# Retention gates: which are projected by four-by-seven blocks, where the retained output is scaled, and how PSUM is divided in the retention stage

## The chip, the core and the metric

The kernel runs on one core of one Trainium2 chip. The metric is device time in microseconds; lower is better. The engines that matter are TensorE (PE in the profile, with its weight loads as PEld), VectorE (DVE), ScalarE (ACT), GpSimd (POOL) and SyncE (SP, which here only issues DMAs). Each works through its own instructions in program order and waits on the others by semaphores.

## The reference

The block is a decoder layer for 1024 tokens of width 1024, in float32. What matters here is the retention branch of its token mixer (4 heads, query and key width 256, value width 512, chunks of 128 tokens):

```python
s = jnp.einsum('bhid,bhjd->bhij', qi, ki) * inner_decay[None]
o = (jnp.einsum('bhij,bhje->bhie', s, vi)
     + jnp.einsum('bhid,bhde->bhie', qi, state) * q_decay[None, :, :, None])
state = (state * chunk_decay[None, :, None, None]
         + jnp.einsum('bhjd,bhje->bhde', ki * k_decay[None, :, :, None], vi))
...
mu = jnp.mean(ro, axis=-1, keepdims=True)
var = jnp.mean(jnp.square(ro - mu), axis=-1, keepdims=True)
ro = (ro - mu) * lax.rsqrt(var + GN_EPS)
ro = ro * gn_g + gn_b
ret_out = (jax.nn.silu(rg) * ro) @ w_ret_out
```

`rg` is a projection of the normed input by 2048 columns: 512 for each head, that is four blocks of 128 channels by 1024 tokens for each head, sixteen in all. Around it stand a dilated attention branch with its own projections, two sigmoid gates, an output projection and a squared-ReLU MLP.

## The kernel before

**Products.** Every float32 product is made of three passes of TensorE over halves of higher and lower precision (`mm3`, L203: low weight times high data, high times low, high times high). Nearly every matmul is 128 by 128 weights against 512 columns.

**Two ways to project.** A block of 128 channels can be projected directly: eight steps over the input width, each of three passes over two halves of the tokens, so 48 matmuls (`proj_mm`, L472). Or two such blocks are done together as a two-by-two block product with seven products instead of eight (class `Blocks`, L226). Each of the seven products has four steps of three passes, so a pair takes 84 matmuls where the direct way takes 96. Those pairs run in the stage `queries_keys` (L1259), one after the other in the order of the string at L1159: `r` retention queries and keys, `a` attention queries, `g` gates, `k` keys, `s` retention gates. For each product `prep` sums weight blocks on DVE and splits them on ACT and DVE, and `post` combines PSUM banks on ACT and DVE. A finished pair goes to DRAM. From `MOD0` on, `mod_turn` (L1243) also loads one modulation column block at a time and reduces it on DVE.

**The retention stage.** `chunk` (L715) runs 32 times, g = 0 to 31, four heads h of eight chunks c. In the order written out by hand, a chunk does on PE: the two `kv` products of the state (six matmuls); some steps of a direct gate projection (`rg_mm`, L695; the table `RG` gives how many steps each chunk takes, and one step is six matmuls); the scores of the next chunk and its transposed keys (`s_kt`, L630); the output `o` (three or nine matmuls); the four transposes of the chunk before (`on_T`, L670); and one last gate step. Around these:

- `kv` is added to the state on DVE (L745), copied to its high half on ACT (L749) and its low half on DVE (L750).
- the scores go through ACT and DVE (L652 to L668), the keys through ACT (L663) and DVE (L666).
- `o` goes through mean and variance on DVE (L772, L773), a scale and shift on DVE (L774), a power on POOL (L775), another product on DVE (L776), and DVE then writes the scaled output `on` (L778).
- `on_T` transposes `on` on PE and four ACT copies (L679) put it in tiles of 128 channels by 1024 tokens.
- `u_final` (L681) runs in the first four chunks of the next head: for each of four channel blocks two ACT instructions with scale and bias (L688), one DVE product with the gate (L690), one DMA (L691). For the last head it runs inside the first attention step (`att_step`, L1831), with its DMAs on POOL's queue.
- `ahead` prepares the next chunk's gate weights, if it has any: an ACT cast (L197) and a DVE subtraction (L198), and the load of a later weight block.

Twelve of the sixteen gate blocks are projected here, three for each head; the other four are two `s` pairs, and `rg_out` (L705) loads one of them for each head.

**PSUM.** There are eight banks of 512 float32 columns. In the retention stage two slots `mm` of two banks hold gate projections, and four slots `s` of one bank take in turn the scores, the transposed keys, the two `kv`, `o` and the transposes.

Of the kernel before, what the change touches and what calls it, by code (L numbers as in the profile page):

```python
# [17 lines left out]
P = 128  # L18
# [21 lines left out]
CS_KDEC = 128  # L40
CS_QD = 132
CS_QD2 = 136
CS_ONE = 140
# [97 lines left out]
def block_kernel(ctx, tc, io, stop=None, dbg=None):  # L141
# [11 lines left out]

    def banks(single):

        if PS:
            PS["ctx"].close()
        PS["i"] = PS.get("i", 0) + 1
        PS["ctx"] = ExitStack()
        PS["p"] = PS["ctx"].enter_context(tc.tile_pool(name=f"psum{PS['i']}", bufs=2, space=bass.MemoryType.PSUM,  # L160
                                                       reuse_waits="tile"))
        PS["n"] = 8 if single else 4

    banks(True)

    def ps_mm(name):
        return PS["p"].tile([P, 2, 512], F32, tag="mm", bufs=2, name=name)

    def ps_s(name, shape=(P, 512)):
# [342 lines left out]
    def etile(name, dt=F32):  # L512
        return R["p"].tile([P, 1024], dt, tag="E", bufs=12, name=name)

# [114 lines left out]

    def s_kt(i):  # L630

# [5 lines left out]
        for i in range(2):  # L637
# [27 lines left out]
        if pk is not None:  # L665
            nc.vector.scalar_tensor_tensor(flat(kl), flat(pk), kd, fv(flat(kh)), op0=ALU.mult, op1=ALU.subtract)  # L666
            hd["k", g] = (kh, kl)
        nc.vector.tensor_sub(sml, sm, fv(smh))  # L668

    def on_T(h, c):  # L670

        po = ps_s(f"oT{h}{c}", (P, 4, P))
        on = hd["o", h, c]
        if c == 0:
            hd["on", h] = [etile(f"on{h}{e}") for e in range(4)]
        for e in range(4):
            nc.tensor.transpose(po[:, e, :], on[:, e * P:(e + 1) * P], ident)
        for e in range(4):
            nc.scalar.copy(hd["on", h][e][:, c * C:(c + 1) * C], po[:, e, :])  # L679

    def u_final(h, es=range(4), queue=nc.sync):  # L681
        for e in es:
            i = h * 4 + e
            t = hd["on", h][e]
            for hf in range(2):
                neg = 16 if hf == i % 2 else 0
                b = t[:, 512 * hf:512 * hf + 512]
                nc.scalar.activation(b, b, AF.Identity, scale=gnv[0][:, neg + i:neg + i + 1],  # L688
                                     bias=gnv[1][:, neg + i:neg + i + 1])
            nc.vector.tensor_mul(t, t, hd["srg", h, e])  # L690
            queue.dma_start(y_d[h][:, 2 * (i % 2):2 * (i % 2) + 2, e // 2], t.rearrange("p (t x) -> p t x", t=2))  # L691

    RG = ((6, 2, 2, 3, 3, 3, 3, 2),) + ((3,) * NC,) * (H - 1)

    def rg_mm(n):  # L695

        for _ in range(n):
            if hd.get("rgk", NK) == NK:
                hd["rgk"], hd["rgw"], hd["rgp"] = 0, hd["rgws"].pop(0), ps_mm("rg")
            proj_mm(hd["rgp"], hd["rgw"], [hd["rgk"]])  # L700
            hd["rgk"] += 1
            if hd["rgk"] == NK:
                hd["rgs"] = hd["rgp"]

    def rg_out(h, c):  # L705

        if "rgs" in hd:
            e = {1: 0, 2: 0, 4: 1, 5: 1, 7: 2}[c]
            hd["srg", h, e] = etile(f"srg{h}{e}")
            nc.scalar.activation(hd["srg", h, e], flat(hd.pop("rgs")), AF.Silu)  # L710
        if c == 6:
            hd["srg", h, 3] = etile(f"srg{h}3")
            nc.sync.dma_start(hd["srg", h, 3], srg_d[h])

    def chunk(h, c, ahead, w=None):  # L715
# [19 lines left out]
        if g == 0:  # L735
            s_kt(1)
        rg_mm(1 if g == 0 else RG[h][c] - 1)
        for i, kv in enumerate(kvs):
# [5 lines left out]
            else:  # L744
                nc.vector.scalar_tensor_tensor(st[:, i, :], st[:, i, :], float(GAMMA[h] ** C), kv,  # L745
                                               op0=ALU.mult, op1=ALU.add)
        if g > 0:
            for i in range(len(kvs)):
                nc.scalar.copy(sh1[:, i, :], st[:, i, :])  # L749
                nc.vector.tensor_sub(sl1[:, i, :], st[:, i, :], fv(sh1[:, i, :]))  # L750
# [15 lines left out]
        if g > 0:  # L766
            on_T(*divmod(g - 1, NC))
        rg_mm(0 if g == 0 else 1)
        bn = p.tile([P, 6], F32, tag="bn", bufs=2, name=f"bn{h}{c}")
        ba = p.tile([P, 2], F32, tag="ba", bufs=2, name=f"ba{h}{c}")  # L770
        gr = p.tile([P, 1], F32, tag="gr", bufs=2, name=f"gr{h}{c}")
        nc.vector.bn_stats(bn, po)  # L772
        nc.vector.bn_aggr(ba, bn)  # L773
        nc.vector.tensor_scalar(gr, ba[:, 1:2], ct[:, CS_QD2 + h:CS_QD2 + h + 1], GN_EPS, op0=ALU.mult, op1=ALU.add)  # L774
        nc.gpsimd.tensor_tensor(gr, gr, mhalf[:, 0:1], op=ALU.pow)  # L775
        nc.vector.tensor_mul(gr, gr, ct[:, CS_QD + h:CS_QD + h + 1])  # L776
        on = p.tile([P, DV], F32, tag="on", bufs=1, name=f"onm{h}{c}")
        nc.vector.tensor_scalar(on, po, ba[:, 0:1], gr, op0=ALU.subtract, op1=ALU.mult)  # L778
        hd["o", h, c] = on
        rg_out(h, c)  # L780
        if h > 0 and c < 4:
            u_final(h - 1, (c,))

# [6 lines left out]
    ak_d = {(p, a): dram.tile([P, S], F32, name=f"akd{p}{a}") for p in range(2) for a in range(2)}  # L790
    srg_d = [dram.tile([P, S], F32, name=f"srgd{h}") for h in range(H)]
    h12_d = [dram.tile([P, 2, 512], F32, name=f"h12d{m}") for m in range(4)]
# [332 lines left out]
    def sums_of_h(name, ms=range(4)):  # L1125

        for m in ms:
# [18 lines left out]
            if name != "t4":  # L1146
# [42 lines left out]
    def a_out(q, n, x, y=None):  # L1189
# [19 lines left out]
        if n in ("12", "21"):  # L1209
            if pair[0] == "g":  # L1210
                dst = gate_d[GATES[2 * pair[1] + i]]
            elif pair[0] == "a":
                dst = aq_d[pair[2], pair[1], i]
            elif pair[0] == "k":
                dst = ak_d[pair[2], i]
            elif pair[0] == "s":
                dst = srg_d[2 * pair[1] + i]
            else:
                return
            nc.sync.dma_start(dst, OA[q][i])  # L1220
# [163 lines left out]
    def values(ahead):  # L1384
# [47 lines left out]
    steps.add(queries_keys, manual=True)  # L1432

    for h in range(H):
        for c in range(NC):
            steps.add((lambda h, c: lambda ahead, *w: chunk(h, c, ahead, *w))(h, c),
                      ([wsplit(io["w_rg"][3 * h + (0, 2, 5).index(c)])] if c in (0, 2, 5) else []),
                      manual=True)
# [392 lines left out]
    def att_step(pair, a):  # L1831

        def body(*args):
            ps = ps_mm(f"ak{pair}1{a}")
            gen = with_sums(proj_gen(ps, args[-1]))
            if a == 1:
                weave(gen, NK, scores_gen(pair, 1, 0), len(SB[1]), lag=2)
            elif pair == 0:
# [4 lines left out]
                drain(gen)  # L1843
                u_final(H - 1, queue=nc.gpsimd)
                for h in range(H):
# [982 lines left out]
def _constants():  # L2828
# [9 lines left out]
    for h in range(H):  # L2838
        lg = math.log(GAMMA[h])
        decay[:, h * C:(h + 1) * C] = \  # L2840
            np.where(i[None, :] >= i[:, None], np.exp(-lg * (i[:, None] + 1)), 0.0) / 16.0
        cst[:, CS_KDEC + h] = np.exp(lg * (C - 1 - i)) / 16.0
        cst[:, CS_QD + h] = np.exp(lg * (i + 1))
        cst[:, CS_QD2 + h] = np.exp(2 * lg * (i + 1))
    cst[:, CS_ONE] = 1.0
# [18 lines left out]
def pack(x, c, w_ada, b_ada, norm1_g, w_in, rel_bias, ret_gn_g, ret_gn_b,  # L2864
# [16 lines left out]
        "w_rv": _vblocks(w[:, 2048:4096]),  # L2881
        "w_rg": _cols(w[:, 4096:6144].reshape(1024, 4, 4, P)[:, :, :3].reshape(1024, 1536)),
        "w_rg2": _pairs(w[:, 4096:6144].reshape(1024, 4, 4, P)[:, :, 3].reshape(1024, 512)),
        "w_aq": _pairs(att[:, :, 0].reshape(1024, 1536)),
# [32 lines left out]
```

## Time and profile before

| what | us |
|---|---|
| time, median of the runs | 2175.16 |
| lowest | 2175.04 |
| the profiled execution's own time | 2173.28 |
| its span, first to last instruction | 2171.3 |
| PE busy | 2144.7 |
| DVE busy | 1520.4 |
| ACT busy | 959.3 |
| POOL busy | 165.7 |

The profile has one row for each instruction with its start and its duration. A row of PE is longer than the time until the next matmul may start, because matmuls are pipelined: how fast PE goes is read from the distance between starts. A group row adds up all instructions of one line, operands and shape: busy microseconds, mean nanoseconds of one, and the idle time of the engine just ahead of them with what ended it.

### The profile page before, as it was taken

How to read it: one execution, taken by the hardware profiler on the slowest of the kernel's cores; microseconds unless marked ns; L12 is line 12 of the kernel's file. 1: busy time of each engine (PE TensorE's matmuls, PEld its weight loads, DVE VectorE, ACT ScalarE, POOL GpSimd, SP SyncE). 2: the span in 40 equal slices, each digit the busy share in tenths (PEclk: the TensorE clock that was granted, in tenths of full speed). 3: DMA queues.
4: the chain of work that ended last, by engine and by line, in shares of the span. 5: the costliest groups of instructions: out<-in, count | busy, mean ns of one | idle time of the engine just before them, and what ended most of it. 6: DMA issues, size and time to landing. Idle time of an engine off the chain costs nothing. (4 is left out here: it accounts for less than half of the span.)

```text
span 2171.3 us, 27289 instructions
## 1 busy us (share of the span) xinstructions
PE 2144.7 (99%) x10036; PEld 1782.4 (82%) x10036; DVE 1520.4 (70%) x2358; ACT 959.3 (44%) x1757; POOL 165.7 (8%) x199
## 2 busy tenths in 40 slices
PE   8999999999999999999999999999999999999998
PEld 6888888888887788888888888888778888888887
DVE  6886777777656677776667644677876665877855
ACT  5543322323334455556656625434454455533413
POOL 0001111100001112211110000001000000000003
PEclk9999999999999999999999999999999999999999
DMA  9859998835588744436877366653144435645322
GB/s 383 282 208 309 285 306 265 243 117 194 186 301 303 234 148 151 160 127 197 218 194 196 115 245 211 217 191 132 64 175 160 150 136 193 253 135 173 109 88 78
DMA packets 162674, 425.18 MB, mean 196 GB/s; under 512 B 28005, under 2 KB 55916, under 8 KB 159468
## 3 DMA queue, kind: packets, MB, share of 16 engines
q1 hardware_dynamic: 150264, 374.90, 48.3%
q0 software_dynamic: 9584, 48.24, 9.9%
q8 instruction: 79, 1.29, 0.2%
q10 hardware_dynamic: 2692, 0.30, 0.1%
q14 instruction: 55, 0.45, 0.1%
HBM read 324.13 MB, written 160.32 MB: 223 GB/s over the span
## 5 line engine op out<-in xcount | busy, mean ns | idle before, releaser
L207 PE MATMUL qap<-hh,qaw 128*128 128x512 f32 x264 | 102.7, 389 | 0.0
L209 PE MATMUL qap<-hl,qaw 128*128 128x512 f32 x264 | 102.7, 389 | 0.0
L211 PE MATMUL qap<-hh,qaw 128*128 128x512 f32 x264 | 102.7, 389 | 0.0
L617 POOL TENSOR_TENSOR j<-qk,j 128x512 fp32r<-128x512 f32 x32 | 42.8, 1338 | 454.8 <-ACT j L616 454.8
L2235 POOL TENSOR_TENSOR accnf<-accnf,sqnf 128x256 f32<-128x256 f32 (+1 forms) x18 | 16.6, 922 | 609.6 <-ACT sqnf L2231 609.6
L2339 ACT ACTIVATE a<-a 128x512 f32<-128x512 f32 x48 | 30.3, 631 | 72.8 <-DVE a L2338 71.3
L749 ACT CAST stateh<-state 128x512 fp32r<-128x512 f32 x54 | 32.9, 622 | 57.8 <-DVE state L745 55.7
L209 PEld LDWEIGHTS qap<-hl,qaw 128*128 128x128 f32 x264 | 49.5, 188 | 10.4
L211 PEld LDWEIGHTS qap<-hh,qaw 128*128 128x128 f32 x264 | 49.6, 188 | 10.3
L207 PEld LDWEIGHTS qap<-hh,qaw 128*128 128x128 f32 x264 | 49.5, 188 | 10.2
L2547 ACT CAST w2h<-w2s 128x512 fp32r<-128x512 f32 x36 | 22.4, 621 | 80.3 <-DVE w2s L2585 80.3
L264 DVE TENSOR_TENSOR fw<-w1r,fw 128x512 fp32r<-128x512 f32 x48 | 32.9, 688 | 33.6 <-ACT fw L254 33.6
L264 DVE TENSOR_TENSOR qaw<-wa,qaw 128x512 fp32r<-128x512 f32 x66 | 44.0, 687 | 9.4 <-ACT qaw L254 9.4
L2070 DVE TENSOR_TENSOR rwl<-rwl,rwh 128x1024 fp32r<-128x1024 f32 x25 | 30.2, 1221 | 29.0 <-ACT rwh L2100 29.0
L207 PE MATMUL fp<-h2h,fw 128*128 128x512 f32 x128 | 50.0, 390 | 0.0
L209 PE MATMUL fp<-h2l,fw 128*128 128x512 f32 x128 | 49.8, 389 | 0.0
L211 PE MATMUL fp<-h2h,fw 128*128 128x512 f32 x128 | 49.8, 389 | 0.0
L207 PE MATMUL roa<-rh,rwl 128*128 128x512 f32 x128 | 49.8, 389 | 0.0
L209 PE MATMUL roa<-rl,rwh 128*128 128x512 f32 x128 | 49.8, 389 | 0.0
L211 PE MATMUL roa<-rh,rwh 128*128 128x512 f32 x128 | 49.8, 389 | 0.0
L1603 ACT ACTIVATE P<-P,ng 128x128 f32<-128x128 f32 (+1 forms) x96 | 41.9, 438 | 17.6 <-DVE ng L1595 17.5
L292 DVE TENSOR_TENSOR qat<-qat,qap 128x512 f32<-128x512 f32 x22 | 15.1, 688 | 42.8 <-PE qap L211 35.8
(3089 smaller groups left out, 7187.8 us busy)
## 6 DMA issues: line engine op xcount, KB each, us to landing
cossin<-in_w_ada_dram SPq DMA_DIRECT2D x32, 512.0 KB, 3.5
v<-vd SPq DMA_DIRECT2D x32, 512.0 KB, 4.3
w1r<-in_w_ff_dram SPq DMA_DIRECT2D x32, 512.0 KB, 4.6
yt<-y POOLq DMA_DIRECT2D x24, 512.0 KB, 7.5
xsd<-as SPq DMA_DIRECT2D x24, 512.0 KB, 3.1
w2r<-in_w_ff2s_dram SPq DMA_DIRECT2D x24, 512.0 KB, 6.4
em<-in_w_ada_dram SPq DMA_DIRECT2D x16, 512.0 KB, 10.2
wrvs<-in_w_rv_dram POOLq DMA_DIRECT2D x16, 512.0 KB, 9.8
```

Of the source, the lines that this page charges most:

```text
L207: nc.tensor.matmul(o, wl, xh, start=first, stop=False, skip_group_check=skip)
L209: nc.tensor.matmul(o, wh, xl, start=False, stop=False, skip_group_check=skip)
L211: nc.tensor.matmul(o, wh, xh, start=False, stop=last, skip_group_check=skip)
L264: nc.vector.tensor_sub(t[:, 512:], src, fv(t[:, :512]))
L292: nc.vector.tensor_sub(u, u, b)
L617: nc.gpsimd.tensor_sub(t[:, 1], src, fv(t[:, 0]))
L749: nc.scalar.copy(sh1[:, i, :], st[:, i, :])
L1603: nc.scalar.activation(v, v, AF.Exp, bias=ng[:, blk:blk + 1], accum_out=st[:, g, blk, 2 + a:3 + a])
L2070: nc.vector.tensor_sub(lo, fv(lo), fv(hi))
L2235: (nc.vector if f == 7 else nc.gpsimd).tensor_add(G["acc", key], G["acc", key], sq)
L2339: nc.scalar.activation(o, o, AF.Relu)
L2547: nc.scalar.copy(hi, src)
```

## The change

Eight gate blocks instead of twelve are projected directly in the retention stage (two for each head), and eight instead of four in pairs, so there are four `s` pairs instead of two; `rg_out` loads two blocks for each head. The table `RG` is rewritten: 64 steps in all instead of 96. The PSUM of the retention stage is divided into three slots `rg` of one bank, two slots `o` of one bank and three slots `s`; `s_kt` puts the transposed keys into the second half of the bank that holds the scores. `on` is written by ACT straight from PSUM, with a scale and a bias that POOL finishes (two more small POOL products), and the factor of the decay is folded into the epsilon. The scale and bias of the group norm move from `u_final` into the copies of `on_T`. `u_final` works on halves of 512 tokens, one in each chunk, and the last head's in eight pieces. `ahead` moves behind the statistics of `o`, and the low halves of the state are written later, one inside `s_kt` and one behind the statistics. `mod_turn` advances once every 2 turns instead of every 16/7. PSUM is divided anew at the first attention step.

```diff
-        PS["n"] = 8 if single else 4
+        PS["n"] = 8 if single else 3 if ret else 4
...
+    def ps_rg(name):
+        return PS["p"].tile([P, 512], F32, tag="rg", bufs=3, name=name)
+
+    def ps_o(name):
+        return PS["p"].tile([P, 512], F32, tag="o", bufs=2, name=name)
...
-    def s_kt(i):
+    def s_kt(i, mid=None):
...
-        pk = ps_s(f"kT{h}{c}", (P, 2, P)) if c < NC - 1 else None
+        pk = ps[:, 2 * C:].rearrange("p (a b) -> p a b", a=2) if c < NC - 1 else None
...
+        if mid:
+            mid()
         nc.vector.tensor_sub(sml, sm, fv(smh))
...
         for e in range(4):
-            nc.scalar.copy(hd["on", h][e][:, c * C:(c + 1) * C], po[:, e, :])
...
+            neg = 16 if c // 4 == i % 2 else 0
+            nc.scalar.activation(hd["on", h, c // 4][e][:, c % 4 * C:(c % 4 + 1) * C], po[:, e, :], AF.Identity,
+                                 scale=gnv[0][:, neg + i:neg + i + 1], bias=gnv[1][:, neg + i:neg + i + 1])
+
+    def u_final(h, e, hf, queue=nc.sync):
+
+        i = h * 4 + e
+        t = hd["on", h, hf][e]
+        nc.vector.tensor_mul(t, t, hd["srg", h, e][:, 512 * hf:512 * hf + 512])
+        queue.dma_start(y_d[h][:, 2 * (i % 2) + hf, e // 2], t)
...
-    RG = ((6, 2, 2, 3, 3, 3, 3, 2),) + ((3,) * NC,) * (H - 1)
+    RG = (6, 2, 2, 1, 2, 1, 2, 3), (3, 2, 2, 2, 2, 2, 1, 3), (2, 2, 2, 1, 2, 2, 1, 3), (2, 2, 1, 2, 2, 1, 1, 2)
...
+                i = hd["rgi"] = hd.get("rgi", -1) + 1
+                t = hd["srg", i // 2, i % 2] = etile(f"srg{i // 2}{i % 2}")
+                for j, ps in enumerate(hd["rgp"]):
+                    nc.scalar.activation(t[:, 512 * j:512 * j + 512], ps, AF.Silu)
...
-        ahead(2)
+        if g == NG - 1:
+            ahead(2)
         if 0 < g < NG - 1:
-            s_kt(g + 1)
-        po = ps_s(f"o{h}{c}")
+            s_kt(g + 1, (lambda: low(0)) if kvs else None)
+        po = ps_o(f"o{h}{c}")
...
-        nc.vector.tensor_scalar(gr, ba[:, 1:2], ct[:, CS_QD2 + h:CS_QD2 + h + 1], GN_EPS, op0=ALU.mult, op1=ALU.add)
-        nc.gpsimd.tensor_tensor(gr, gr, mhalf[:, 0:1], op=ALU.pow)
-        nc.vector.tensor_mul(gr, gr, ct[:, CS_QD + h:CS_QD + h + 1])
+        nc.vector.tensor_scalar_add(gr[:, 0:1], ba[:, 1:2], ct[:, CS_EQ + h:CS_EQ + h + 1])
+        nc.gpsimd.tensor_tensor(gr[:, 2:3], ba[:, 0:1], ct[:, CS_NEG:CS_NEG + 1], op=ALU.mult)
+        nc.gpsimd.tensor_tensor(gr[:, 1:2], gr[:, 0:1], mhalf[:, 0:1], op=ALU.pow)
+        nc.gpsimd.tensor_tensor(gr[:, 2:3], gr[:, 1:2], gr[:, 2:3], op=ALU.mult)
+        if g > 0 and kvs:
+            low(1)
+        if g < NG - 1:
+            ahead(2)
+        if h > 0:
+            u_final(h - 1, c // 2, c % 2)
         on = p.tile([P, DV], F32, tag="on", bufs=1, name=f"onm{h}{c}")
-        nc.vector.tensor_scalar(on, po, ba[:, 0:1], gr, op0=ALU.subtract, op1=ALU.mult)
+        nc.scalar.activation(on, po, AF.Identity, scale=gr[:, 1:2], bias=gr[:, 2:3])
...
-    s_pairs = [("s", i) for i in range(H // 2)]
+    s_pairs = [("s", i) for i in range(H)]
...
-             for i in "rargrarkrargrarkgagass"]
+             for i in "rargrarkrargrarkgagassss"]
...
-        while turn["i"] < NV + 2 and 7 * turn["n"] > 16 * turn["i"]:
+        while turn["i"] < NV + 2 and turn["n"] > 2 * turn["i"]:
...
-        banks(False)
+        banks(False, True)
...
+            if pair == a == 0:
+                banks(False)
...
-                u_final(H - 1, queue=nc.gpsimd)
+                for e in range(4):
+                    for hf in range(2):
+                        u_final(H - 1, e, hf, nc.gpsimd)
```

More of the change, by code (lines that the diff above doesn't have):

```diff
@@ L152, in block_kernel, with banks @@
     PS = {}
-    def banks(single):
+    def banks(single, ret=False):
         if PS:
@@ L512, in etile @@
     def etile(name, dt=F32):
-        return R["p"].tile([P, 1024], dt, tag="E", bufs=12, name=name)
+        return R["p"].tile([P, 1024], dt, tag="E", bufs=5, name=name)
     y_d = [dram.tile([P, 4, 2, 512], F32, name=f"y{h}") for h in range(H)]
@@ L673, in on_T @@
         on = hd["o", h, c]
-        if c == 0:
-            hd["on", h] = [etile(f"on{h}{e}") for e in range(4)]
+        if c % 4 == 0:
+            hd["on", h, c // 4] = [R["p"].tile([P, 512], F32, tag="EO", bufs=13, name=f"on{h}{c}{e}") for e in range(4)]
         for e in range(4):
@@ L702, in rg_mm @@
             if hd["rgk"] == NK:
-                hd["rgs"] = hd["rgp"]
+                i = hd["rgi"] = hd.get("rgi", -1) + 1
+                t = hd["srg", i // 2, i % 2] = etile(f"srg{i // 2}{i % 2}")
+                for j, ps in enumerate(hd["rgp"]):
+                    nc.scalar.activation(t[:, 512 * j:512 * j + 512], ps, AF.Silu)
     def rg_out(h, c):
-        if "rgs" in hd:
-            e = {1: 0, 2: 0, 4: 1, 5: 1, 7: 2}[c]
+        if c in (4, 6):
+            e = c // 2
             hd["srg", h, e] = etile(f"srg{h}{e}")
[L710 to L713, printed above, removed]
+            nc.sync.dma_start(hd["srg", h, e], srg_d[h, e - 2])
     def chunk(h, c, ahead, w=None):
@@ L736, in chunk @@
             s_kt(1)
-        rg_mm(1 if g == 0 else RG[h][c] - 1)
+        rg_mm(1 if g == 0 else RG[h][c] - (g < NG - 1))
         for i, kv in enumerate(kvs):
@@ L790, in block_kernel @@
     ak_d = {(p, a): dram.tile([P, S], F32, name=f"akd{p}{a}") for p in range(2) for a in range(2)}
-    srg_d = [dram.tile([P, S], F32, name=f"srgd{h}") for h in range(H)]
+    srg_d = {(h, i): dram.tile([P, S], F32, name=f"srgd{h}{i}") for h in range(H) for i in range(2)}
     h12_d = [dram.tile([P, 2, 512], F32, name=f"h12d{m}") for m in range(4)]
@@ L1216, in a_out @@
             elif pair[0] == "s":
-                dst = srg_d[2 * pair[1] + i]
+                dst = srg_d[pair[1], i]
             else:
@@ L1432, in block_kernel @@
     steps.add(queries_keys, manual=True)
+    RGW, n = [], 0
+    for g in range(NG):
+        RGW += [g - (g > 1)] * (n < 8 * len(RGW) + 1 <= n + RG[g // NC][g % NC])
+        n += RG[g // NC][g % NC]
     for h in range(H):
```

39 lines of the change are left out of this document (14 added, 25 removed).

## The prediction

> **What bounds the kernel now.** The page comes first: the span, the busy time of each engine, the granted clock.
>
> ```profile
> span 2171.3 us, 27289 instructions
> ...
> PE 2144.7 (99%) x10036; PEld 1782.4 (82%) x10036; DVE 1520.4 (70%) x2358; ACT 959.3 (44%) x1757; POOL 165.7 (8%) x199
> ...
> PEclk9999999999999999999999999999999999999999
> ```
>
> PE is busy throughout at full clock; no other engine is close. But a busy PE is only an upper bound on work, so I look next at the two stages that the change touches. The view of stretches gives, for each window, its length and then busy time and instruction count of PE, PEld, DVE, ACT and POOL: the seven-product stage, the retention stage, and one retention chunk inside it.
>
> ```profile
> 180.00:600.00 420.00, 420.00 (x1855) 347.77 (x1854) 307.23 (x477) 124.25 (x216) 36.33 (x50) 1.00 0.75 233
> 712.40:980.70 268.30, 266.76 (x1316) 221.37 (x1317) 197.34 (x417) 141.01 (x352) 54.84 (x62) 1.00 0.48 158
> 859.65:868.29 8.64, 8.64 (x44) 7.23 (x43) 7.06 (x14) 5.53 (x13) 1.80 (x2) 1.00 0.62 212
> ```
>
> In the first, 1855 matmuls of 512 columns fill 420 us without a gap: one every 226 ns. In the second PE idles 1.5 of 268 us. So in both stages time is matmuls times their spacing, as long as DVE (74% in retention) and ACT (53%) keep up. What PE waits for at all, from the view of waits for PE (total, times, longest):
>
> ```profile
> PE rg L207 <- DVE vr L1367: 1.1, 1, 1.1
> ...
> PE kv L207 <- ACT state L763: 0.9, 1, 0.9
> ...
> PE sc L209 <- DVE kl L1544: 0.4, 1, 0.4
> ...
> PE o L207 <- DVE state L745: 0.2, 1, 0.2
> ```
>
> These four are nearly all the waits in and around the retention stage: 2.6 us together. There is almost nothing to win there except by taking matmuls away, and the reader should keep in mind the opposite: each chunk that gets shorter on PE leaves DVE and ACT less time to be ready.
>
> **The matmuls.** Two more pairs are added to the seven-product stage. Their price is the distance from one pair to the next; the view by tile shows the same product, "s1", of pairs 0 and 1.
>
> ```profile
> L207 PE MATMUL qap<-xat,qaw0s x12: 389/389/389, 182.4 to 189.9; 128*128 128x512 f32 x12
> ...
> L207 PE MATMUL qap<-xat,qaw1s x12: 389/389/389, 201.5 to 209.0; 128*128 128x512 f32 x12
> ```
>
> From 182.4 to 201.5 is 19.1 us for 84 matmuls (227 ns each), so two pairs add 38.2 us. Taken away are four directly projected blocks, that is 32 steps of `rg_mm` (96 less 64). In order of time, on PE, in the retention chunk of above:
>
> ```profile
> 865.58 0.62 PE L207 MATMUL rg<-hh,raw_6203l 128*128 128x512 f32 x2
> ...
> 866.93 0.62 PE L207 MATMUL rg<-hh,raw_6203l 128*128 128x512 f32 x2
> ...
> 868.29 0.28 PE L638 MATMUL sT<-j 128*128 128x256 f32 x1
> ```
>
> One step goes from 865.58 to 866.93: 1.35 us; two go from 865.58 to 868.29: 2.71. `RG` takes them nearly all from this place behind `kv` (the step behind the transposes stays), so 32 steps are 43.4 us. The sum on PE is 38.2 - 43.4 = -5.2 us; counted as 168 matmuls more and 192 fewer at 227 ns it is -5.4. I take -5.3. The duration column (389 ns) would have given 24 x 389 = 9.3 us, and is wrong for this, because two matmuls overlap in it.
>
> [...]
>
> The new pairs need, on the other engines, what the present ones do: DVE is 73% busy in that stage, and PE never waits for it. `s` pairs lack the rotation that `r` pairs carry. `mod_turn` at every 2 turns instead of 16/7 adds a DVE reduction for about one turn in sixteen, beside PE. Two pairs also load and store 4 MB more, but four weight blocks fewer are loaded later: DMA is at 0.75 of its share in a stage where PE waits for nothing. I cost all this at nothing; were that cover gone, one late block would cost one product's worth, about 2.7 us.
>
> **DVE and ACT in the shorter chunks.** A chunk with all its parts takes 8.64 us with three steps, hence 7.3 with two and 5.9 with one. `RG` has eight chunks of one step, never more than two in a row, and two heads begin with a chunk that has two steps but no state products, also 5.9 (8.64 - 1.35 - 6 x 0.227): ten short chunks. The groups of the retention stage, by line, give what each engine must do in that time (count, busy us, mean ns):
>
> ```profile
> L749 ACT CAST stateh<-state 128x512 fp32r<-128x512 f32 x54 | 32.9, 622 | 57.8 <-DVE state L745 55.7 <-DVE state L743 2.0
> L778 DVE TENSOR_SCALAR onm<-o,ba,gr 128x512 f32<-128x512 f32 x32 | 25.9, 810 | 3.4
> L679 ACT COPY on<-oT 128x128 f32<-128x128 f32 x128 | 24.6, 277 | 17.2 <-PE oT L677 17.2
> L688 ACT ACTIVATE on<-on,gnt 128x512 f32<-128x512 f32 x25 | 19.4, 838 | 0.0
> L690 DVE TENSOR_TENSOR on<-on,srg 128x1024 f32<-128x1024 f32 x12 | 14.6, 1219 | 0.1
> L710 ACT ACTIVATE srg<-rg 128x1024 f32<-128x1024 f32 x12 | 12.6, 1050 | 3.1 <-PE rg L211 3.1
> L653 DVE TENSOR_TENSOR sm<-sm,sT 128x128 f32<-128x128 f32 x32 | 9.1, 284 | 19.1 <-ACT sm L652 19.1
> L776 DVE TENSOR_TENSOR gr<-gr,ct 128x1 f32<-128x1 f32 x32 | 5.1, 160 | 28.2 <-POOL gr L775 28.2
> ```
>
> and the same chunk in order of time on DVE, ACT and POOL:
>
> ```profile
> 861.77 1.23 DVE L198 TENSOR_TENSOR raw_6386l<-raw,raw_6386h 128x1024 fp32r<-128x1024 f32 x1 [0.25 <-ACT raw_6386h L197]
> 864.10 0.69 DVE L772 BATCH_NORM_STATS2 bn<-o 128x6 f32<-128x512 f32 x1
> 866.29 0.16 DVE L776 TENSOR_TENSOR gr<-gr,ct 128x1 f32<-128x1 f32 x1 [1.03 <-POOL gr L775]
> 868.42 1.28 DVE L745 SCALAR_TENSOR_TENSOR state<-state,kv 128x512 f32<-128x512 f32 x2
> ```
> ```profile
> 860.70 1.04 ACT L197 CAST raw_6386h<-raw 128x1024 fp32r<-128x1024 f32 x1
> 864.28 0.76 ACT L679 COPY on<-oT 128x128 f32<-128x128 f32 x4
> 864.91 1.55 ACT L688 ACTIVATE on<-on,gnt 128x512 f32<-128x512 f32 x2
> ```
> ```profile
> 864.46 1.30 POOL L617 TENSOR_TENSOR j<-qk,j 128x512 fp32r<-128x512 f32 x1 [7.76 <-ACT j L616]
> 865.71 0.55 POOL L775 TENSOR_TENSOR gr<-gr,ct 128x1 f32<-128x1 f32 x1
> ```
>
> *DVE* loses L778 (0.81), L776 (0.16) and, what is more, the wait for POOL ahead of L776 (28.2 us in all). The product with the gate comes in halves of some 0.69 us in every chunk instead of 1.22 in every second. Its 7.06 us in this chunk become 7.06 - 1.23 (weights) - 0.81 - 0.16 - 1.22 + 0.69, plus some 0.8 of the state update that falls outside the window here: 5.1 us, or 6.4 in the seven chunks that prepare weights. A short chunk has 5.9. Two of those prepare weights: one is in the first head, which has no gate product to do, and the other follows a head's last chunk, which has no state update.
>
> *ACT* gets `on` and the scaled copies, and loses L688. With two operand columns L688 takes 838 ns, where the plain cast of the same size takes 622: 216 ns more. For a copy of 128 columns the trace has 277 without them; bounds are 277 and 838, I take 277 + 216 = 493. Back to back, four copies take 0.76 now (about 0.35 of overlap), then 1.6. For `on` the bounds are 622 and 838; I take 0.8. So ACT's 5.53 us here become 5.53 - 1.55 - 1.04 (weights) + 0.85 + 0.8 = 4.6, and 5.7 with either a gate's activation (L710, 1.05) or a weight cast. That is under 5.9 too, but only just.
>
> *The new wait* is `on`: ACT now waits for POOL, where DVE did. POOL does three small products of 0.55 behind the 1.30 of L617 instead of one. Statistics take about 1.2 us from the end of `o`, POOL 1.7 more, `on` 0.8: some 4 us, or 5 if a gate's activation and a weight cast stand ahead. Its reader, `on_T` of the next chunk on PE, comes one chunk length after, 5.9 us at the least. Behind `on` in ACT's queue are the next chunk's casts of the state (L749), not due before `kv` and DVE's update have run, 3.4 us after `o`. So PE has one to two microseconds in hand; I put the short chunks at 0.1 us each, 1 us in all. The bounds are 0 and 1.1 us for each of the ten.
>
> On SP, stores of `u_final` (24 halves instead of 12) wait for DVE ahead of the loads of the chunk after next but one; those have two chunks to spare.
>
> **PSUM.** `o` gets its own banks, which ends its wait for a bank that `kv` held (the 0.2 us with L745 above). Three slots instead of four serve `kv`, scores and transposes; each is read within a chunk, and I cost this at nothing. The last head's eight ACT instructions (L688, 0.7 us apart) leave ACT's queue ahead of the first attention keys, which should remove the 0.4 us before `sc`. I take -0.5 for both.
>
> [...]
>
> **The sum.** -5.3 - 0.5 + 1.0 = -4.8 us on the profiled execution's own 2173.28 (span 2171.3 and 2.0 around it): 2168.5. The median of the runs, 2175.16, lies 1.9 above that execution, so I predict 2170.4 for the median.
>
> **The rivals.**
>
> 1. *More comes back* (0.14). DVE stops waiting for POOL, so nearly all of the 2.6 us of waits go and the short chunks cost nothing: -5.3 - 2.5, 2167.4. For it: DVE's 28.2 us of waits. Against: two of the four waits belong to the stage's start, which changes little.
> 2. *ACT becomes the bound of the short chunks* (0.16): slower than before. Its place is the queue from the scaled copies over the gate's activation to `on`. If short chunks need 7.0 us instead of 5.9 (4.6 with a gate's activation, a weight cast and a wait of 0.3), ten times 1.1 is 11: -5.3 + 11 = +5.7, 2180.9. It decides from about 0.5 us for each short chunk. If every one of the 32 chunks lost 1.5 us it would be 2% (0.02).
> 3. *The shared bank is guarded as a whole* (0.08). ACT's key cast waits for L653 and its hand-over, 0.28 us in 28 chunks, 7.8 us if ACT is the last to be ready: 2177.7. If it isn't, nothing. [...]
> 4. *The saving doesn't arise* (0.04): the added pairs run into DVE or into late weights, 2.7 us for each. Then it is 2175. Against it: no gap in 420 us of the same work.
>
> The forecast itself has 0.58 (0.01 of that for a gain of over 2% by something I don't see). **Range**: 2164 to 2181. It takes in the forecast, the first, third and fourth rivals and the second but for its tail. 2% (43 us) is about what a measurement of this kernel can tell from no change; every case but the last part of rival 2 is inside: faster 0.01, same 0.97, slower 0.02.
>
> **What would show it.** Matmuls of the whole kernel fall by 24. The seven-product stage grows by 38 us without gaps; the retention stage shrinks from 268 to about 225. ACT's rows: scaled copies near 0.49, `on` near 0.8. Waits of PE on `on`, `kh`, `kl` or the state stay under 1 us each. What would make it wrong: PE waits in short chunks that add up to over 5 us (ACT at over 90% there), or a first attention step that waits for the newly divided PSUM.

## The result and the profile after

The kernel after takes 2197.55 us, median of its runs (2193.91 to 2197.82), against 2175.1 of the kernel before beside it: a ratio of 1.0101, 95% interval 1.0089 to 1.0114. That is 1% slower; the forecast was 2170.4 and the range ended at 2181. One of the four executions of the kernel before took 2676.74 us, far from the other three, and is left out of the ratio. The profiled execution took 2197.82. Its page:

```profile
span 2196.0 us, 27432 instructions
...
PE 2153.8 (98%) x10012; PEld 1778.0 (81%) x10012; DVE 1530.9 (70%) x2338; ACT 983.4 (45%) x1781; POOL 199.3 (9%) x267
```

There are 24 matmuls fewer, and yet PE is busy 9 us longer and DVE 10 us. The stretches of the seven-product stage, and of the retention stage from its first gate matmul to the first attention matmul (length, then PE, PEld, DVE, ACT and POOL busy, granted clock, DMA share, GB/s):

```profile
180.00:637.00 457.00, 457.00 (x2018) 378.39 (x2017) 336.36 (x525) 137.45 (x240) 36.23 (x50) 1.00 0.75 233
749.30:1002.80 253.50, 235.25 (x1126) 182.35 (x1124) 186.32 (x361) 155.82 (x360) 87.55 (x123) 0.99 0.50 161
```

The first window is drawn 37 us longer and is as full as before; from its own first matmul to the first of the next stage, the seven-product stage grew by 38.1 us, the two pairs' price. The second should have come to 268.3 - 43.4 = 224.9 and came to 253.5: **28.6 us were lost in the retention stage**, and the whole miss, 2197.82 - 2168.5 = 29.3, is nearly that. PE idles 18.3 us of it. What it waits for most in that stage (total, times, longest):

```profile
PE rg L213 <- ACT srg L712: 5.3, 5, 2.5
...
PE kv L213 <- DVE kl L672: 5.0, 10, 0.7
PE oT L685 <- DVE state L751: 2.4, 3, 1.0
PE ak L213 <- DVE raw_7272l L204: 1.9, 1, 1.9
```

Three of the four end in a DVE row. DVE's busy time in the stage, 186.3, ought to have fallen well below that of before (197.3) with 56 rows fewer. By tile, count and min/median/max in ns, the scores' low half in the kernel before:

```profile
L668 DVE TENSOR_TENSOR sml<-sm,smh x32: 291/293/294, 717.2 to 971.7; 128x128 fp32r<-128x128 f32 x32
```

and the same line, POOL's power and ACT's `on` in the kernel after:

```profile
L676 DVE TENSOR_TENSOR sml<-sm,smh x32: 279/1381/1389, 754.4 to 996.0; 128x128 fp32r<-128x128 f32 x32
...
L785 POOL TENSOR_TENSOR gr<-gr,ct x32: 538/922/1001, 763.2 to 1004.0; 128x1 f32<-128x1 f32 x32
...
L794 ACT ACTIVATE onm<-o,gr x32: 777/779/782, 765.1 to 1005.3; 128x512 f32<-128x512 f32 x32
```

The same subtraction of the same shape takes 1.38 us instead of 0.29. Its row of the groups has 34.3 us where 32 x 0.293 would be 9.4: 25 us of DVE's time. The power takes 0.92 instead of 0.55. One chunk of the kernel after, in order of time:

```profile
922.79 0.29 DVE L660 TENSOR_TENSOR sm<-sm,decay 128x128 f32<-128x128 f32 x1
922.79 0.47 ACT L669 ACTIVATE kh<-sT,ct 128x256 fp32r<-128x256 f32 x1 [0.35 <-DVE sm L659]
...
923.30 0.48 DVE L672 SCALAR_TENSOR_TENSOR kl<-sT,ct,kh 128x256 fp32r<-128x256 f32 x1 [0.21 <-ACT kh L669]
...
923.70 0.68 DVE L754 TENSOR_TENSOR statel<-state,stateh 128x512 fp32r<-128x512 f32 x1
...
924.05 1.48 POOL L623 TENSOR_TENSOR j<-qk,j 128x512 fp32r<-128x512 f32 x1 [3.62 <-ACT j L622]
924.30 1.38 DVE L676 TENSOR_TENSOR sml<-sm,smh 128x128 fp32r<-128x128 f32 x1
```

POOL's subtraction begins at 924.05, while the moved low half of the state is on DVE; `sml` is next on DVE, at 924.30, and ends at 925.68, just after POOL has (925.53). So it is in 23 of the 32 chunks, where `sml` starts inside POOL's subtraction: 1.38 us. In the other nine it starts outside and takes 0.28.

What that does to a chunk is read from one chunk's statistics on DVE to the next's. Two neighbours in the last head, the first with 38 matmuls, the second with one gate step less:

```profile
974.78:982.52 7.74, 7.55 (x38) 5.67 (x36) 6.36 (x14) 4.56 (x11) 2.79 (x4) 1.00 0.43 135
982.52:990.26 7.74, 6.94 (x32) 4.67 (x32) 6.36 (x13) 4.55 (x11) 2.80 (x4) 1.00 0.31 105
```

By the prediction's count PE needs 7.3 and 5.9 us for a chunk of two steps and of one. Both last 7.74: DVE's round, its 6.36 us of rows and the time between them, sets the length and not PE.

### The profile page after: what moved, and what is told of

Read it like the earlier page. It is cut to its first block, busy times and chain, and to the rows that moved or that the text cites. A ratio compares the mean times of both kernels' runs of the same rounds, so it can differ in the third digit from the quotient of the medians.

```text
span 2196.0 us, 27432 instructions
## 1 busy us (share of the span) xinstructions
PE 2153.8 (98%) x10012; PEld 1778.0 (81%) x10012; DVE 1530.9 (70%) x2338; ACT 983.4 (45%) x1781; POOL 199.3 (9%) x267
## 3 DMA queue, kind: packets, MB, share of 16 engines
q8 instruction: 79, 1.29, 0.2%
## 5 line engine op out<-in xcount | busy, mean ns | idle before, releaser
L215 PE MATMUL qap<-hl,qaw 128*128 128x512 f32 x288 | 112.0, 389 | 0.0
L213 PE MATMUL qap<-hh,qaw 128*128 128x512 f32 x288 | 112.0, 389 | 0.0
L217 PE MATMUL qap<-hh,qaw 128*128 128x512 f32 x288 | 112.0, 389 | 0.0
L215 PEld LDWEIGHTS qap<-hl,qaw 128*128 128x128 f32 x288 | 54.1, 188 | 11.2
L213 PEld LDWEIGHTS qap<-hh,qaw 128*128 128x128 f32 x288 | 54.1, 188 | 11.2
L217 PEld LDWEIGHTS qap<-hh,qaw 128*128 128x128 f32 x288 | 54.1, 188 | 11.2
L794 ACT ACTIVATE onm<-o,gr 128x512 f32<-128x512 f32 x32 | 24.9, 779 | 68.3 <-POOL gr L786 68.3
L689 ACT ACTIVATE on<-oT,gnt 128x128 f32<-128x128 f32 x128 | 48.1, 460 | 5.0 <-PE oT L685 5.0
```

The costliest lines, as they stand in the source:

```text
L213: nc.tensor.matmul(o, wl, xh, start=first, stop=False, skip_group_check=skip)
L215: nc.tensor.matmul(o, wh, xl, start=False, stop=False, skip_group_check=skip)
L217: nc.tensor.matmul(o, wh, xh, start=False, stop=last, skip_group_check=skip)
L689: nc.scalar.activation(hd["on", h, c // 4][e][:, c % 4 * C:(c % 4 + 1) * C], po[:, e, :], AF.Identity, scale=gnv[0][:, neg + i:neg + i + 1 ...
L794: nc.scalar.activation(on, po, AF.Identity, scale=gr[:, 1:2], bias=gr[:, 2:3])
```

## The experiments

Three theories stood at first. The moved low half brings `sml` behind POOL, and DVE's lost time is the loss (A); ACT waits for POOL ahead of `on`, 66 us in all, and that is the loss (B); or the chunks are simply too short for the work of the other engines (C). A ratio is to the kernel before on the same chip, with its 95% interval; a difference between two runs is that of their medians. "Stage" is the retention stage from its first gate matmul to the first attention matmul: 268.3 before, 253.5 after, 224.9 by the count of matmuls.

**First run: the kernel before with the gate blocks divided anew.** `RG` is the table of the change, `s` pairs are four; nothing else.

```diff
-    RG = ((6, 2, 2, 3, 3, 3, 3, 2),) + ((3,) * NC,) * (H - 1)
+    RG = (6, 2, 2, 1, 2, 1, 2, 3), (3, 2, 2, 2, 2, 2, 1, 3), (2, 2, 2, 1, 2, 2, 1, 3), (2, 2, 1, 2, 2, 1, 1, 2)
-    s_pairs = [("s", i) for i in range(H // 2)]
+    s_pairs = [("s", i) for i in range(H)]
```

> The kernel before, with the gates divided as in the change (eight blocks by seven products, 64 steps in the retention stage, the change's table) and nothing else of it. If the loss lies in the rewritten chunk (theories A and B below), this is what the prediction counted: 5 us faster than before, 2170, with PE waiting under 3 us in the retention stage. If short chunks lose by themselves whatever their order (theory C), PE waits 10 us or more in them and the time is 2180 or above.

2190.74 us, 1.0065 [1.0048, 1.0081]; stage 249.8. What PE waits for most (total, times, longest):

```profile
PE o L207 <- DVE state L746: 11.0, 17, 1.3
```

With the old order of DVE and the old banks, `o` waits 17 times for a bank that DVE has yet to read. So short chunks do run into DVE unless DVE's work is taken away too.

**Second run: the kernel after with `sml` ahead of the moved low half.**

```diff
-        if mid:
-            mid()
         nc.vector.tensor_sub(sml, sm, fv(smh))
+        if mid:
+            mid()
```

> The changed kernel with one exchange: the low half of the scores is subtracted before the first low half of the state, not after it. Theory A says that DVE's subtraction of two SBUF operands stands still while POOL works on the queries' and keys' low half: then the row of the scores' low half falls from 1.38 to about 0.3 us, DVE gains up to 25 us of busy time, and the time falls by 8 to 18 us, unless the state's low half now meets POOL in its stead (its row 0.68 becomes 1.5 or more and little is gained). Theory B (ACT held by its wait for POOL ahead of the scaled output) says that little changes: within 4 us of 2197.

2176.44 us, 1.0006 [0.9996, 1.0016]: 21 us come back from two lines changing places, more than expected. The median of `sml` is 0.283. POOL's subtraction now takes a median of 1.68 (1.29 in the kernel before), where it starts 0.15 us inside the low half behind `sml`; that low half keeps its 0.68, so it is POOL that stands. ACT still waits 46 us for POOL ahead of `on`.

**Third run: the kernel after with both low halves of the state straight behind their casts**, ahead of the scores, as in the kernel before.

```diff
                 nc.scalar.copy(sh1[:, i, :], st[:, i, :])
+            for i in range(2):
+                low(i)
-            s_kt(g + 1, (lambda: low(0)) if kvs else None)
+            s_kt(g + 1)
-        if g > 0 and kvs:
-            low(1)
```

> The changed kernel with both low halves of the state written where they stood before, right behind ACT's casts of the state and ahead of the next chunk's scores. Theory A: no subtraction of two SBUF operands is left beside POOL's, the scores' low half costs 0.3 us, POOL's power 0.55 instead of 0.92, and the time falls by 10 to 20 us, to 2178 to 2188. Theory B: ACT still waits about 60 us for POOL, and the time stays above 2190.

2173.72 us, 0.9997 [0.9988, 1.0007]; stage 232.3: 24 us come back, where 10 to 20 were expected. `sml` 0.28, the power 0.54. ACT still waits 24 us for POOL. The chunks without weights are shorter than in the kernel after:

```profile
953.95:960.75 6.80, 6.80 (x36) 5.65 (x35) 5.48 (x14) 4.66 (x12) 2.58 (x4) 1.00 0.48 153
```

PE's largest wait in the stage is now at the end of gate blocks:

```profile
PE rg L213 <- ACT srg L712: 4.7, 6, 2.9
```

**Fourth run: the kernel after with the scaled output on DVE again.** This takes away ACT's wait for POOL and leaves the order of the low halves.

```diff
-        nc.scalar.activation(on, po, AF.Identity, scale=gr[:, 1:2], bias=gr[:, 2:3])
+        nc.vector.tensor_scalar(on, po, gr[:, 1:2], gr[:, 2:3], op0=ALU.mult, op1=ALU.add)
```

> The changed kernel with the scaled output written by DVE (0.8 us, with the same scale and bias from POOL) instead of ACT. Theory B: ACT no longer waits 68 us for POOL, so casts of the state, the scores and the gates' activations come in time, and the time falls by 10 us or more. Theory A: DVE is the late engine; it gets 0.8 us and a wait more in each chunk, and the time rises to 2205 or more.

2210.95 us, 1.0163 [1.0146, 1.0181], slower than the kernel after. PE waits:

```profile
PE kv L213 <- DVE kl L672: 12.1, 19, 0.7
PE oT L685 <- DVE state L751: 10.1, 12, 1.6
```

ACT's waits for POOL fall from 66 to 8 us and the time rises. This edit also gives DVE 0.8 us more in each chunk, so alone it doesn't speak against theory B. With the second run it does: there ACT still waits 46 us for POOL, and 21 us came back. B is not the main loss; the late engine is DVE.

**Fifth run: the kernel before with the moved low half alone.** The first low half of the state goes between the keys' low half and `sml`, as in the change.

```diff
-    def s_kt(i):
+    def s_kt(i, mid=None):
...
+        if mid:
+            mid()
         nc.vector.tensor_sub(sml, sm, fv(smh))
```

> The kernel before with one instruction moved: the first low half of the state is written inside the next chunk's scores, ahead of the scores' low half, as the change has it. Nothing else. Theory A (DVE's subtraction of two SBUF operands stands behind POOL's): the scores' low half goes from 0.29 to about 1.4 us in two chunks of three or more, DVE's busy time grows by about 25 us, and with long chunks (three steps) PE loses part of it: 2 to 15 us. If A is wrong, the row stays at 0.29 and the time within 2 us of before.

2175.83 us, 1.0004 [0.9994, 1.0013]: a miss for theory A as I had it. The median of `sml` stays at 0.283, and its longest is 0.293. In order of time:

```profile
863.53 0.29 DVE L654 TENSOR_TENSOR sm<-sm,decay 128x128 f32<-128x128 f32 x1
863.74 0.47 DVE L666 SCALAR_TENSOR_TENSOR kl<-kT,ct,kh 128x256 fp32r<-128x256 f32 x1
...
864.14 0.68 DVE L758 TENSOR_TENSOR statel<-state,stateh 128x512 fp32r<-128x512 f32 x1
...
864.74 0.28 DVE L670 TENSOR_TENSOR sml<-sm,smh 128x128 fp32r<-128x128 f32 x1
864.75 1.42 POOL L617 TENSOR_TENSOR j<-qk,j 128x512 fp32r<-128x512 f32 x1 [7.75 <-ACT j L616]
```

Here `sml` is first, by 0.01 to 0.02 us, in most chunks. In the kernel after POOL is first by 0.25. In these runs the order alone does not decide; who comes first does.

**Sixth run: the first run with the PSUM of the change** (own banks for gates and `o`, scores and keys in one slot).

```diff
-        pk = ps_s(f"kT{h}{c}", (P, 2, P)) if c < NC - 1 else None
+        pk = ps[:, 2 * C:].rearrange("p (a b) -> p a b", a=2) if c < NC - 1 else None
-        po = ps_s(f"o{h}{c}")
+        po = ps_o(f"o{h}{c}")
```

> The kernel with the new division of the gates alone (2191), and the change's division of PSUM besides: banks of their own for gates and for the output, the transposed keys in the scores' bank. Order of the chunk, scaled output and pieces of the last product as before. If its loss is the output waiting for a bank that the state update still reads (11 us of waits of PE on DVE's state), it falls to 2170 to 2178. If DVE is late whatever the banks, PE waits for keys or transposes instead and it stays above 2184.

2195.21 us, 1.0089 [1.0074, 1.0104]; `sml` 0.28. The waits for banks are gone and another is in their place:

```profile
PE kv L213 <- DVE kl L672: 15.2, 17, 2.0
```

With the output still on DVE the stage stays at 249.8 and 254.5, 25 to 30 us above the count, whatever the banks: theory C holds for that order of the work.

**Seventh run: the third with the output on DVE.**

> The changed kernel with early low halves (2174) and the scaled output written by DVE instead of ACT. What is the change's move of the output to ACT worth once DVE doesn't stand behind POOL? If DVE still is the engine that the short chunks wait for, it rises by 8 us or more. If ACT's wait for POOL (24 us) holds the gates' activations, PE's 4.7 us of waits on them go, and it falls by 2 to 5.

2191.43 us, 1.0074 [1.0059, 1.0089], 17.7 above the third run, with `sml` at 0.28 and PE's waits again on the keys:

```profile
PE kv L213 <- DVE kl L672: 8.3, 10, 1.2
```

Moving the scaled output to ACT is thus what lets the short chunks pay; that part of the change did what the prediction's DVE sum took it for.

**Eighth run: the third with two rows of `RG` changed**, so that no gate block ends in chunk 6.

```diff
-    RG = (6, 2, 2, 1, 2, 1, 2, 3), (3, 2, 2, 2, 2, 2, 1, 3), (2, 2, 2, 1, 2, 2, 1, 3), (2, 2, 1, 2, 2, 1, 1, 2)
+    RG = (6, 2, 2, 2, 2, 2, 1, 2), (3, 2, 2, 2, 2, 2, 1, 3), (2, 2, 2, 2, 2, 2, 1, 2), (2, 2, 1, 2, 2, 1, 1, 2)
```

> The changed kernel with early low halves, and two rows of the table of gate steps changed so that no gate block ends in a head's chunk 6, behind which no state product separates it from the next block's first matmul. Same number of steps. PE's two long waits on the gate's activation (1.3 and 3.0 us) should go, with the half-speed matmuls behind the longer one: 3 to 6 us less than 2174, 2168 to 2171, faster than both kernels. If the waits move to the next block's end, nothing is gained.

2170.24 us, 0.9981 [0.9972, 0.9990]: faster than both kernels. Stage 229.3. PE waits there:

```profile
PE kv L213 <- DVE kl L672: 1.3, 2, 1.1
PE ak L213 <- DVE raw_7272l L204: 1.3, 1, 1.3
...
PE rg L213 <- ACT srg L712: 0.8, 4, 0.2
```

A block that ends in chunk 6 has its next block's steps right behind it, since chunk 7 has no state products; with three gate banks the second half of the new block waits until ACT has activated the first half of the old one. The third run's wait on `srg`, 4.7 us, is now 0.8, and the time fell by 3.5. The new rows have six chunks of one step instead of eight as well; what that is worth by itself was not measured, but PE's wait on the keys hardly moves (1.4 us in the third run, 1.3 here). The half-speed matmuls that I had expected to remove aren't in the third run (last section).

**Ninth run: the kernel before with two edits, the moved low half and the shared slot of scores and keys.** Long chunks, old banks, output on DVE.

```diff
-        pk = ps_s(f"kT{h}{c}", (P, 2, P)) if c < NC - 1 else None
+        pk = ps[:, 2 * C:].rearrange("p (a b) -> p a b", a=2) if c < NC - 1 else None
...
+        if mid:
+            mid()
         nc.vector.tensor_sub(sml, sm, fv(smh))
```

> The kernel before with two parts of the change: the first low half of the state moved ahead of the scores' low half (as in the fifth run), and scores and transposed keys in one PSUM slot. Everything else is as before, long chunks included. Theory A2 (the shared slot puts ACT's key cast behind DVE's first addition of the scores, so DVE's low half of the keys and the moved low half of the state come later against ACT's cast of j, and POOL's subtraction begins ahead of DVE's low half of the scores): that subtraction has a median near 1.4 us, with over 16 of 32 inside POOL's subtraction, and POOL's power goes above 0.6 us; the time is 2175 to 2185, since the long chunks leave DVE room. Theory A3 (it also needs the short chunks and the late output): the subtraction stays at 0.28 us and the time at 2175 to 2177.

2198.29 us, 1.0107 [1.0092, 1.0122]. The collision is there, 23 of 32 at 1.38 us, and costs more than I expected; the power on POOL stays at 0.54, where I had expected over 0.6. In order of time:

```profile
802.72 0.29 DVE L654 TENSOR_TENSOR sm<-sm,decay 128x128 f32<-128x128 f32 x1
802.72 0.47 ACT L663 ACTIVATE kh<-sT,ct 128x256 fp32r<-128x256 f32 x1 [1.33 <-DVE sm L653]
...
803.23 0.48 DVE L666 SCALAR_TENSOR_TENSOR kl<-sT,ct,kh 128x256 fp32r<-128x256 f32 x1 [0.22 <-ACT kh L663]
...
803.98 1.48 POOL L617 TENSOR_TENSOR j<-qk,j 128x512 fp32r<-128x512 f32 x1 [7.79 <-ACT j L616]
804.23 1.38 DVE L670 TENSOR_TENSOR sml<-sm,smh 128x128 fp32r<-128x128 f32 x1
...
812.36 0.29 DVE L654 TENSOR_TENSOR sm<-sm,decay 128x128 f32<-128x128 f32 x1
```

Count from L654, the product with the decay. In the fifth run `kl` comes 0.21 us later, `sml` 1.21, POOL 1.22. Here ACT's key cast starts only at 802.72, behind DVE's addition (1.33 us of idle time end there), so `kl` comes at 0.51, `sml` at 1.51 and POOL at 1.26. The kernel after has 0.51, 1.51 and 1.26 too. The slot moves DVE by 0.30 us against ACT's cast of `j`, and that is enough. From 802.72 to 812.36 a chunk lasts 9.64 us where it took 8.64. DVE has 7.87 us of rows in it and 1.57 of waits for ACT and POOL between them, so its round is now longer than PE's. The stretch, and what PE waits for:

```profile
802.72:812.36 9.64, 8.59 (x43) 7.16 (x43) 7.87 (x15) 4.65 (x13) 2.03 (x2) 1.00 0.42 135
```
```profile
PE kv L207 <- DVE kl L666: 17.6, 14, 2.2
```

**Tenth run: the kernel after with POOL's subtraction replaced by a fill with zeros.** It leaves out the low halves of the queries and keys.

```diff
-        nc.gpsimd.tensor_sub(t[:, 1], src, fv(t[:, 0]))
+        nc.gpsimd.memset(fv(t[:, 1]), 0.0)
```

> The kernel after, with POOL's subtraction for the low half of the prepared queries and keys replaced by a fill with zeros, which reads nothing from SBUF. So the low halves of the queries and keys are left out of the scores and of the state's product; matmuls, casts and every other instruction stay, in the same order. Theory A (DVE's subtraction of two SBUF tiles stands still while POOL reads SBUF): the subtraction goes from 1.38 to about 0.28 us although it is behind the moved low half as in the kernel after, POOL's power falls to about 0.55, and the time falls to 2172 to 2179, about the second run's. Theory D (it is the place in the order, or the state's low half ahead of it, that makes the subtraction long, whatever POOL does): it stays near 1.38 us and the time near 2195.

2170.72 us, 0.9985 [0.9974, 0.9996], 27 us under the kernel after and below the 2172 to 2179 expected, with every DVE row in the same order. First `sml` by tile, then the fill in order of time:

```profile
L676 DVE TENSOR_TENSOR sml<-sm,smh x32: 280/284/287, 753.0 to 971.9; 128x128 fp32r<-128x128 f32 x32
```
```profile
829.90 0.53 POOL L623 MEMSET j<- 128x512 f32 x1 [2.27 <-PE o L217]
829.99 0.29 DVE L660 TENSOR_TENSOR sm<-sm,decay 128x128 f32<-128x128 f32 x1
...
831.50 0.28 DVE L676 TENSOR_TENSOR sml<-sm,smh 128x128 fp32r<-128x128 f32 x1
```

So `sml` stands still because of POOL's subtraction (0.28 us without it, 1.38 with it), and not because of its place in the order. The fill doesn't wait for ACT's cast of `j`, comes earlier, and in no chunk runs beside `sml` itself. But in 11 chunks it runs beside the product with the decay (L660), a DVE instruction of two SBUF operands as well, which takes 0.29 us in all 32: the fill held none of them.

The power stays at 0.92, against my expectation: POOL is there mostly beside the second low half (L754), not beside `sml`. The fill is also shorter, 0.53 us instead of a mean of 1.43, which helps POOL to start the statistics; so the 27 us are not all the standing still of `sml`.

**Eleventh run: the kernel before with the shared slot alone.**

> The kernel before with scores and transposed keys in one PSUM slot, and nothing else of the change. Theory A2 (the slot does harm only through the order: it shifts DVE's chain 0.30 us against ACT's cast of j, which matters only with a low half of the state ahead of the scores' low half): ACT's key cast waits for DVE's addition as in the ninth run, the subtraction of the scores' low half stays at 0.28 to 0.29 us with 0 of 32 inside POOL's subtraction, and the time is 2174 to 2179. Theory S (the shared slot is what costs the ninth run its 22 us, by ACT's wait on DVE in every chunk): 2190 or more, with the subtraction at 0.28 us.

2174.62 us, 0.9999 [0.9989, 1.0008]; `sml` at 0.281. ACT's key cast waits for DVE's addition in 28 chunks, as in the ninth run, and it costs nothing.

| the kernel before with | us | ratio | median of `sml`, us |
|---|---|---|---|
| moved low half | 2175.83 | 1.0004 | 0.28 |
| shared slot | 2174.62 | 0.9999 | 0.28 |
| both | 2198.29 | 1.0107 | 1.38 |

## Why the prediction was wrong

**The step that failed** stands in the part on DVE and ACT in the shorter chunks: DVE's 5.1 us. It was made from the durations of the kernel before, as if an instruction kept its length where it was put, and it said nothing of the low halves "written later" at all; they were moved at no cost. With the collision the subtraction alone costs 25 us of DVE in 23 chunks, long ones included: in the two chunks shown DVE has 6.36 us of rows instead of 5.1. The step also compared DVE's busy time with the length of a chunk and left out the waits between DVE's rows; with them the round is 7.74 us, more than a chunk of two steps needs (7.3), not only one of 5.9. Without the collision (third run) it is 6.80, with 5.48 of rows, so most of the 5.1 was right there. In the sum, the term that failed is the 1.0 us for ten short chunks, where the stage lost 28.6; its bounds of 0 and 1.1 us for each were bounds for another mechanism. (By the same count the last chunk, of two steps and no state products, is an eleventh; that would be 0.1 us.)

Two facts were in the trace of before and were not put together. POOL's subtraction reads two SBUF tiles for 1.30 us behind ACT's cast of `j`, and `sml`, two SBUF tiles too, ran 0.57 us ahead of it. The moved low half takes 0.60 of DVE's time there (864.14 to 864.74), which leaves `sml` just ahead of POOL; the 0.30 of the slot put it behind. For a plain DVE instruction of two SBUF operands beside POOL the runs show three cases: 1.38 us where POOL's subtraction was first by 0.25 (the kernel after and the ninth run), 0.28 where DVE was first by 0.01 (the fifth), and 0.29 for the product with the decay beside a POOL that only writes (the tenth). The prediction weighed none of this.

**Rival 3** had its chain right and its price wrong. No row of before could show ACT's key cast behind DVE's addition, since the keys had a slot of their own there; in the kernel after it waits so in 28 chunks, 9.9 us in all (0.35 in the chunk shown). By itself that is free, as the eleventh run shows; I priced it as 7.8 us of direct delay, and in the ninth run it cost 22 us, through `sml`.

**Rival 2** placed the trouble on ACT. PE does wait for the gate's activation (5.3 us), and ACT does wait 66 us for POOL. But with that wait gone the time rose (fourth run), and with the collision gone by order (third run) the time is that of before, though ACT still waits 24 us for POOL. What was ACT's own is the ends of two blocks in chunk 6, up to 3.5 us in the eighth run. I had looked for short chunks, and not at what stands behind a block's end.

**What was right.** The seven-product stage grew from 418.9 to 457.0 from its first matmul to that of the next stage, 38.1 against 38.2, without gaps. There are 24 matmuls fewer. The scaled copies take 460 ns (493 predicted), `on` 779 (800). PE no longer waits for a bank ahead of `o`, nor ahead of the first attention scores; but the first attention step now waits 1.9 us for weights that DVE splits late (`ak` above). The saving did arise on PE, against rival 4; rival 1, that more would come back, had no room once DVE was late. With the collision gone and the blocks ended elsewhere, the stage is at 229.3, 4.4 us above the count, where the prediction had allowed about 1; so the 0.1 us for a short chunk was low even then. That the eighth run's 2170.24 stands beside the forecast of 2170.4 doesn't bear the prediction out: it is another kernel, with two more edits, and the two numbers meet by luck.

**What stays open.** Of the 28.6 us, 18.3 are PE's idle time; the rest is spread over rows that count as busy but stand further apart, and was not followed row by row. The kernel after with scores and keys in slots of their own was not tried: its eight banks are all given out (three `rg`, two `o`, three `s`).

## What to carry to other kernels

A duration from a trace holds for the neighbours that the instruction had there: `sml` took 0.29 us in the kernel before and 1.38 in the kernel after. Before moving a DVE instruction with two SBUF operands, look in the order of time for POOL instructions that read SBUF beside its new place, and put it ahead of them or behind their end: here `sml` took 1.38 us where it started inside POOL's subtraction, and 0.28 outside. Compare with the length of a stage's round not an engine's busy time alone but its rows and its waits for the others together. Two edits that are each free (1.0004 and 0.9999 here) may cost 1% together (1.0107) if one moves an instruction to the edge of a race and the other moves the edge; so price them as a pair, and when a loss isn't explained by undoing one, try both alone in the old kernel. Where blocks end, look at what PE does next: a new block straight behind needs its bank from an activation that has just begun (4.7 us of PE's waits on `srg` in the third run, 0.8 in the eighth).

## What the hardware showed that I had not expected

A lead of hundredths of a microsecond was enough, and the outcome repeats: `sml` ahead of POOL by 0.01 to 0.02 us takes its 0.28 (fifth run, none of 32 above 0.293), and POOL ahead by 0.25 holds it for 1.1 us (kernel after, 23 chunks).

PE went at half speed behind some of its waits. In the kernel after, behind waits of 1.0 and 2.5 us within five microseconds, pairs of gate matmuls start 0.85 apart, 427 ns for one instead of 227, for some three microseconds:

```profile
809.56 0.50 PE L213 MATMUL rg<-hh,raw_5634l 128*128 128x512 f32 x1 [2.32 <-ACT srg L712]
...
929.97 0.63 PE L685 MATMUL oT<-ct,onm 128*128 128x128 f32 x4 [1.00 <-DVE state L751]
...
934.68 0.50 PE L213 MATMUL rg<-hh,raw_6592l 128*128 128x512 f32 x1 [2.46 <-ACT srg L712]
...
936.41 1.06 PE L213 MATMUL rg<-hh,raw_6592l 128*128 128x512 f32 x2
937.26 1.06 PE L215 MATMUL rg<-hl,raw_6592h 128*128 128x512 f32 x2
```

Behind the wait of 2.3 us at 809.56 matmuls start 232 ns apart (809.89 to 812.21). The granted clock is 0.50 in the slow stretch, for 3.4 us, and once more at the first attention step, behind a wait of 1.9 us at 1002.80:

```profile
935.40:938.82 3.42, 3.42 (x10) 2.66 (x9) 0.00 (x0) 0.78 (x1) 0.43 (x2) 0.50 0.73 227
1003.70:1007.00 3.30, 3.30 (x10) 2.53 (x9) 0.81 (x2) 1.71 (x2) 1.30 (x3) 0.50 0.73 238
```

In the third run PE waits longer at the same place, 2.9 us, and goes on with 230 ns from start to start:

```profile
919.63 0.50 PE L213 MATMUL rg<-hh,raw_6592l 128*128 128x512 f32 x1 [2.86 <-ACT srg L712]
919.97 0.62 PE L215 MATMUL rg<-hl,raw_6592h 128*128 128x512 f32 x2
920.43 0.62 PE L217 MATMUL rg<-hh,raw_6592h 128*128 128x512 f32 x2
```

The length of the wait alone doesn't decide it: half speed came behind waits of 2.5 and 1.9 us, and not behind those of 2.3 and, in the third run, 2.9. What does is not shown. The first slow stretch cost about 1.6 us by an estimate, 8 matmuls at 0.2 more (427 ns instead of 227), so the wait of 2.5 us was dearer than its own length.
